# Interleaving the two second-level products of a convolution pair, quarter by quarter

## The chip, the cores and the metric

The kernel runs on one core of one Trainium2 chip. The metric is the device time of one execution in microseconds (us), the median of several. Five engines work at once, each through its own queue of instructions in a fixed order: TensorE (PE) multiplies matrices, VectorE (DVE) and ScalarE (ACT) work element by element, GpSimd (POOL) does a little, and SyncE (SP) issues DMAs. PE writes its products to PSUM, here in banks of 512 float32 columns on 128 partitions.

## What is computed

A decoder layer of two branches over 1024 positions of 1024 channels, all in float32. One large projection makes the inputs of gated linear attention (q, k, v, z_a, gates), of a short gated convolution (cb, cc, xc, z_c) and of the merge (g_a, g_c):

```python
h = rms_norm(x, norm_mix_g)
proj = h @ w_in
q, k, v, z_a, gk_low, cb, cc, xc, z_c, g_a, g_c = split(proj)
o = rms_norm(gla_chunked(q, k, v, gates(gk_low)), gla_norm_g)
y_a = (o * silu(z_a)) @ w_branch_a
u = causal_dwconv(cc * xc, conv_w)              # 3 taps along the sequence
y_c = ((cb * u) * silu(z_c)) @ w_branch_c
merged = sigmoid(g_a + b_ga) * y_a + sigmoid(g_c + b_gc) * y_c
x = x + merged @ w_out
x = x + sigmoid(rms_norm(x, norm_ple_g) @ w_ple_gate) * (p @ w_ple_proj)
return rms_norm(x, norm_final_g)
```

## The kernel before

**Products.** A float32 operand is kept as a high and a low part (hi, lo), and a product of two such operands is three matmuls (`mm3`): hi x hi, lo x hi, hi x lo. The projections are made by a Strassen-Winograd scheme: a `Cell` is 256 columns of one weight, and its eight half-size products become seven, numbered 0 to 6. Each is 12 matmuls of 512 columns, called a wide product here. A cell has three PSUM banks X, Y and V (`cc2X` is bank X of cell cc2). Product 0 is made in X and copied to Y, product 1 in V; products 2, 4 and 6 add to Y, 3 to X, 5 to V. The cells' weight sums are made by DVE in tiles of the tag "T" (four buffers), and split by ACT (a CAST to the high part) and DVE (the low part) into tiles of a ring of six (`RING`, tags whi and wlo).

**The second level.** `Deep(pair, k, turned, pool)` makes product k (0 or 1) of the two cells of a pair together by the same scheme once more: seven quarter products of six matmuls of 256 columns, into the left and right halves of the two cells' banks. Its weight operands are called A, S, T and B (tiles `cc2xc20Ahi`, `cc2xc21Shi` and so on: cells, k, operand, part). Between the quarter products ACT copies halves from bank to bank or into a tile `dw`, and DVE adds. For product 0 this happens in the X banks, for product 1 in the V banks. The convolution has eight pairs: cc0xc0, zc0cb0, cc1xc1, zc1cb1, cc2xc2, zc2cb2, cc3xc3, zc3cb3. The first has a `Deep` for k = 0 alone, the seven others for both. The pairs q0k0 and q1k1 have one for k = 0, the pairs of g_a and g_c one for k = 1. `run(k)` of a `Deep` makes one of its four stretches: quarter product 0; then 4 and 2; then 1; then 3, 5 and 6.

**Order.** `line_up` writes down the order of products: it inserts the stretches of the second level among the wide products of the pair ahead, one wide product or more between two stretches. `run_groups` walks that list and, ahead of each product, loads weight blocks and prepares operands of the coming ones, as far as the ring reaches, by the `slots` that each takes. Every operation is recorded by `Flow` (nearly all rows of the trace carry the line of its call, L508, so rows are told apart by tile names). `set_dues` works out from the end when each must be done, and `put_in_order` takes, for each engine, the most urgent operation that can run. PE's main row keeps the order in which the code names its products. In the finished program a bank is guarded as a whole: an instruction that uses one half waits for an earlier use of the other half by another engine.

Of the kernel before, what the change touches and what calls it, by code (L numbers as in the profile page):

```python
# [16 lines left out]
P = 128  # L17
# [8 lines left out]
RING = 6  # L26
# [493 lines left out]
def kernel(  # L520
# [219 lines left out]
    class Cell:  # L740

        slots = 1

        def __init__(self, name, side, src, res, cons, prods=ORDER, begin=None, s1=None, u2=None, s5=None, fresh=(), mixed=False):
# [7 lines left out]
            (self.steps, self.operand), self.fresh = ring_steps(name, side, self.raw, fresh, mixed), fresh  # L752

# [57 lines left out]
        def run(self, k):  # L811
# [20 lines left out]
            elif k == 2:  # L832
                self.product(2, self.Y, False)
# [24 lines left out]
    class Deep:  # L858

        slots = 4  # L860

        def __init__(self, pair, k, turned, pool):
            self.pair, self.k, self.turned, self.pool, self.ring, self.behind = pair, k, turned, pool, [], []
            self.first = False
            for c in pair:
                c.deep[k] = self
                c.prods = [n for n in c.prods if n != k]
# [3 lines left out]

        def load(self, k):
            for c in self.pair:
                c.load(self.k)

        def prep(self, k):
            if self.ring:
                return
            for c, n in self.behind:
                c.prep(n)  # L880
            self.load(k)
            a, b = (c.operand(self.k) for c in self.pair)
            name = f"{self.pair[0].name}{self.pair[1].name}{self.k}"

            def put(what, src):
                hi = bp.tile([P, 4, P], F32R, tag="whi", name=f"{name}{what}hi", bufs=RING)
                lo = bp.tile([P, 4, P], F32R, tag="wlo", name=f"{name}{what}lo", bufs=RING)
                n = src.shape[1]
                split(hi[:, 0:n, :], lo[:, 0:n, :], src)
                return [(hi[:, m:m + 2, :], lo[:, m:m + 2, :]) for m in range(0, n, 2)]  # L890

            t = [bp.tile([P, 4, P], F32, tag="T", name=f"{name}S{m}", bufs=4) for m in range(2)]
            s1, s2, s3, s4 = (t[m][:, n:n + 2, :] for m in range(2) for n in (0, 2))
            tt(s3, a[:, 0:2, :], b[:, 0:2, :], op=ALU.subtract)
            tt(s1, b[:, 0:2, :], b[:, 2:4, :], op=ALU.add)
            tt(s2, s1, a[:, 0:2, :], op=ALU.subtract)
            tt(s4, a[:, 2:4, :], s2, op=ALU.subtract)
            a11, a12 = put("A", a)
            s1, s2 = put("S", t[0])
            s3, s4 = put("T", t[1])  # L900
            a22, = put("B", b[:, 2:4, :])
            self.ring = [a11, s3, s2, a12, s1, s4, a22]

        def product(self, n, acc, start):
# [8 lines left out]
        def run(self, k):  # L913
            self.prep(k)
            a, b = self.pair
            left, right = slice(0, 256), slice(256, 512)
            if k == (0 if self.first else 2) and self.k:
                for c in self.pair:
                    c.Y = bank(c, 1)
                    nc.scalar.copy(c.Y, c.X if c.seed is None else c.seed)  # L920
            if k == 0:
# [3 lines left out]
            elif k == 1:  # L925
                self.product(4, self.a[:, right], False)
                self.product(2, self.b[:, left], False)
                self.d = [self.pool.tile([P, 256], F32, tag=f"dw{n}", name=f"{a.name}{self.k}dw{n}") for n in range(2)]
                nc.scalar.copy(self.d[0], self.b[:, left])
                nc.scalar.copy(self.d[1], self.a[:, right])  # L930
                tt(self.a[:, right], self.a[:, right], self.d[0], op=ALU.add)
            elif k == 2:
                self.product(1, self.b[:, left], False)
# [1333 lines left out]
```

## Time and profile before

| | us |
|---|---|
| median of 3 runs | 1067.59 (1066.97 to 1067.98) |
| the profiled execution, its own time | 1067.77 |
| its span | 1065.9 |
| PE busy | 1056.9 (99%) |
| DVE busy | 928.9 (87%) |
| ACT busy | 678.1 (64%) |
| POOL busy | 48.9 (5%) |

The span runs from the first to the last instruction that the profiler saw; 1.87 us lie around it. A row of the timeline gives the start, the duration, the engine, and the operation as out<-in. A matmul's duration includes its way through the array, so matmuls overlap: what counts is the distance between two starts, 0.23 us for 512 columns and 0.12 for 256.

### The profile page before, as it was taken

The numbers are of one execution on the slowest core, as the hardware profiler recorded it, in microseconds if no ns is written. First come the engines' busy times: TensorE is split into PE (matmuls) and PEld (weight loads), VectorE is DVE, ScalarE is ACT, GpSimd is POOL, SyncE is SP. The second block draws the span as 40 slices with busy tenths as digits, with TensorE's granted clock in tenths as the row PEclk, the third lists the DMA queues.
The fourth block names the chain that finished last, engine by engine and source line by source line (L and its number), as shares of the span: only waits on it lengthen the run. The fifth ranks groups of instructions, "written<-read, shape, count | busy, mean of one in ns | idle before, by whom it ended". The sixth has DMA issues, their size and how long they took to land.

```text
span 1065.9 us, 16311 instructions
## 1 busy us (share of the span) xinstructions
PE 1056.9 (99%) x5235; PEld 896.7 (84%) x5235; DVE 928.9 (87%) x1576; ACT 678.1 (64%) x1295; POOL 48.9 (5%) x83
## 2 busy tenths in 40 slices
PE   9999999999999999999999999999999999999997
PEld 7888888888888888888888889988888888888886
DVE  6899869968897898889889799997999989899897
ACT  6867768876545656556566478676857535456656
POOL 0000000000000000000000002120000000012221
PEclk9999999999999999999999999999999999999999
DMA  8996468966768666865869879998596879799963
GB/s 311 331 363 217 181 205 280 314 228 230 232 202 284 225 221 213 263 220 182 275 220 322 289 247 323 320 337 315 197 310 229 314 215 318 251 327 326 315 220 142
DMA packets 179269, 280.18 MB, mean 263 GB/s; under 512 B 15728, under 2 KB 84592, under 8 KB 176752
## 3 DMA queue, kind: packets, MB, share of 16 engines
q1 hardware_dynamic: 179040, 278.89, 77.5%
q8 instruction: 41, 0.67, 0.3%
q14 instruction: 44, 0.36, 0.1%
q10 hardware_dynamic: 144, 0.26, 0.1%
HBM read 178.95 MB, written 100.14 MB: 262 GB/s over the span
## 4 chain that ended last, share of the span: by engine, by line
PE 92%; DVE 3%; DMA 1%; ACT 1%; issue 1%; POOL 0%; POOLq 0%; SPq 0%; ACTq 0%
PE pe L508 2%; PE op L508 2%; PE j0Y L508 1%; PE vY L508 1%; PE zY L508 1%; DMA wt<-in_wb_dram 1%; PE j1X L508 1%; PE j0X L508 1%; PE j0V L508 1%; PE kv L508 1%; PE ga1Y L508 1%; PE xc3Y L508 1%; PE cb2Y L508 1%; PE cb1Y L508 1%; PE cb0Y L508 1%; PE cc3Y L508 1%
## 5 line engine op out<-in xcount | busy, mean ns | idle before, releaser
L508 DVE TENSOR_TENSOR wt<-wt 128x256 f32<-128x256 f32 (+1 forms) x48 | 24.6, 513 | 2.1 <-issue 2.0
L508 ACT ACT_TABLE_LOAD x19 | 24.4, 1283 | 1.3 <-PEq L2256 0.7
L508 DVE SCALAR_TENSOR_TENSOR u<-t,vec,u 128x512 f32<-128x512 f32 x32 | 23.9, 754 | 1.1 <-ACT u L508 0.9
L508 ACT ACTIVATE junk<-x 128x512 bf16<-128x512 f32 (+1 forms) x30 | 18.0, 600 | 10.0 <-DVE x L508 8.2
L508 POOL TENSOR_SCALAR rg<-ms 128x1 f32<-128x1 f32 x8 | 10.2, 1275 | 257.0 <-ACT junk L508 256.9
L508 POOL MEMSET t<- 128x2 f32 x8 | 0.8, 99 | 405.6 <-DMA ked<-turned 202.3
L508 ACT ACTIVATE og<-op,or 128x256 f32<-128x256 f32 x32 | 13.4, 472 | 1.8 <-POOL or L508 1.8
L508 ACT ACTIVATE wt<-wt,vec 128x256 f32<-128x256 f32 x32 | 13.8, 501 | 0.0
L508 ACT ACTIVATE oq<-oq,vec 128x512 f32<-128x512 f32 x20 | 13.2, 715 | 0.3 <-DMA oq<-od 0.3
L508 DVE TENSOR_TENSOR vs<-vs 128x512 fp32r<-128x512 f32 x16 | 11.0, 689 | 2.8 <-ACT vs L508 2.7
L508 ACT CAST S<-S 128x512 fp32r<-128x512 f32 x14 | 8.7, 621 | 7.3 <-PE op L508 7.3
L508 ACT ACTIVATE junk<-op 128x256 bf16<-128x256 f32 x32 | 12.2, 382 | 1.4 <-PE op L508 1.3
L508 ACT ACTIVATE u<-t,vec 128x512 f32<-128x512 f32 x16 | 11.6, 725 | 2.3 <-DVE t L508 2.3
L508 PE MATMUL pe<-wpehi,pThi 128*128 128x512 f32 x32 | 13.0, 408 | 0.0
L508 DVE STREAM_TRANSPOSE oT<-szl 128x256 f32<-128x256 f32 x32 | 13.0, 428 | 0.0
L508 PE MATMUL pe<-wpelo,pThi 128*128 128x512 f32 x32 | 12.9, 404 | 0.0
L508 DVE TENSOR_TENSOR s<-y,s 128x512 f32<-128x512 f32 x16 | 11.0, 689 | 2.2 <-DMA vs<-vd 1.2
L508 PE MATMUL op<-v,aTh 128*128 128x256 f32 x64 | 12.7, 282 | 0.0
L508 ACT CAST vs<-vs 128x512 fp32r<-128x512 f32 x16 | 9.9, 621 | 3.9 <-DMA vs<-vd 3.7
L508 POOL TENSOR_TENSOR or<-or,mhalf 128x2 f32<-128x2 f32 x16 | 12.2, 761 | 1.3
L508 PE MATMUL pe<-wpehi,pTlo 128*128 128x512 f32 x32 | 12.0, 390 | 0.0
L508 DVE SCALAR_TENSOR_TENSOR S<-S,dds,kv 128x256 f32<-128x256 f32 x24 | 10.4, 473 | 1.4 <-PE kv L508 1.2
(4252 smaller groups left out, 4393.6 us busy)
## 6 DMA issues: line engine op xcount, KB each, us to landing
wtd<-wt SPq DMA_DIRECT2D x88, 128.0 KB, 3.0
wt<-in_wb_dram SPq DMA_DIRECT2D x16, 512.0 KB, 5.1
vsd<-vs SPq DMA_DIRECT2D x16, 512.0 KB, 4.2
v<-vsd SPq DMA_DIRECT2D x16, 512.0 KB, 5.6
wgq<-wtd SPq DMA_DIRECT2D x7, 1024.0 KB, 6.5
vraw<-in_wv_dram SPq DMA_DIRECT2D x24, 256.0 KB, 4.1
zraw<-in_wv_dram SPq DMA_DIRECT2D x20, 256.0 KB, 5.1
uq<-ud SPq DMA_DIRECT2D x5, 1024.0 KB, 6.8
```

Source lines behind the costliest of these rows:

```text
L508: o.call(*[place(a) for a in o.args], **{k: place(a) for k, a in o.kw.items()})
```

## The change

`Deep` is split into `begin` (the weight sums), `put` (one operand into the ring) and `step(n)`, one of six steps: 0 is quarter product 0 and the copy of its half bank, 1 is quarter product 4 and a copy to a tile d5, 2 is quarter product 2, a copy to a tile dw and an add, 3 is quarter product 1 and an add, 4 is quarter products 3 and 5, 5 is quarter product 6. A new class `Duo` holds both parts (k = 0 and k = 1) of a pair and makes each step for the one and then for the other, steps 0 to 2 in a first stretch and 3 to 5 in a second. `line_up` puts the first stretch ahead of the last wide product (6) of the pair ahead's first cell and the second ahead of that of its second cell. A `Deep` that is alone has three stretches, (0), (1, 2) and (3, 4, 5). The copy into bank Y moves into product 2 of the cell. A T operand of the first part lies in a tile outside the ring (xhi, xlo), and both B operands share one ring tile. Quarter products, copies and adds are the same in number.

```diff
         def load(self, k):
             for n in NEED[self.side][k]:
@@ -830,6 +831,9 @@
                 if self.X is not None:
                     self.join()
             elif k == 2:
+                if self.Y is None:
+                    self.Y = bank(self, 1)
+                    nc.scalar.copy(self.Y, self.X if self.seed is None else self.seed)
                 self.product(2, self.Y, False)
...
+        def __init__(self, pair, k, turned, pool, home=None):
+            self.pair, self.k, self.turned, self.pool, self.home, self.behind = pair, k, turned, pool, home or pool, []
...
+        def slots(self, k):
+            return 0 if k else 4
...
+        def begin(self):
+            self.load(0)
+            self.ab = a, b = [c.operand(self.k) for c in self.pair]
+            self.t = t = [bp.tile([P, 4, P], F32, tag="T", name=f"{self.name}S{m}", bufs=4) for m in range(2)]
+            s1, s2, s3, s4 = (t[m][:, n:n + 2, :] for m in range(2) for n in (0, 2))
+            tt(s3, a[:, 0:2, :], b[:, 0:2, :], op=ALU.subtract)
+            tt(s1, b[:, 0:2, :], b[:, 2:4, :], op=ALU.add)
+            tt(s2, s1, a[:, 0:2, :], op=ALU.subtract)
+            tt(s4, a[:, 2:4, :], s2, op=ALU.subtract)
+
+        def put(self, what, left, right=None, extra=None):
+            src = {"A": self.ab[0], "S": self.t[0], "T": self.t[1], "B": self.ab[1][:, 2:4, :]}[what]
+            hi = (extra or bp).tile([P, 4, P], F32R, tag="xhi" if extra else "whi", name=f"{self.name}{what}hi", bufs=1 if extra else RING)
+            lo = (extra or bp).tile([P, 4, P], F32R, tag="xlo" if extra else "wlo", name=f"{self.name}{what}lo", bufs=1 if extra else RING)
+            n = src.shape[1]
+            split(hi[:, 0:n, :], lo[:, 0:n, :], src)
+            self.ring[left] = hi[:, 0:2, :], lo[:, 0:2, :]
+            if right is not None:
+                self.ring[right] = hi[:, 2:4, :], lo[:, 2:4, :]
+            return hi, lo
...
-        def run(self, k):
-            self.prep(k)
+        def step(self, n):
             a, b = self.pair
             left, right = slice(0, 256), slice(256, 512)
-            if k == (0 if self.first else 2) and self.k:
-                for c in self.pair:
-                    c.Y = bank(c, 1)
-                    nc.scalar.copy(c.Y, c.X if c.seed is None else c.seed)
-            if k == 0:
+            if n == 0:
                 self.a, self.b = bank(a, 2 * self.k), bank(b, 2 * self.k)
                 self.product(0, self.a[:, left], True)
                 nc.scalar.copy(self.b[:, left], self.a[:, left])
-            elif k == 1:
-                self.product(4, self.a[:, right], False)
-                self.product(2, self.b[:, left], False)
-                self.d = [self.pool.tile([P, 256], F32, tag=f"dw{n}", name=f"{a.name}{self.k}dw{n}") for n in range(2)]
-                nc.scalar.copy(self.d[0], self.b[:, left])
-                nc.scalar.copy(self.d[1], self.a[:, right])
-                tt(self.a[:, right], self.a[:, right], self.d[0], op=ALU.add)
-            elif k == 2:
-                self.product(1, self.b[:, left], False)
-                tt(self.b[:, right], self.b[:, left], self.d[1], op=ALU.add)
+            elif n == 1:
+                self.product(4, self.a[:, right])
+                self.d5 = self.home.tile([P, 256], F32, tag="d5", name=f"{self.name}d5")
+                nc.scalar.copy(self.d5, self.a[:, right])
+            elif n == 2:
+                self.product(2, self.b[:, left])
+                d = self.pool.tile([P, 256], F32, tag="dw", name=f"{self.name}d")
+                nc.scalar.copy(d, self.b[:, left])
+                tt(self.a[:, right], self.a[:, right], d, op=ALU.add)
+            elif n == 3:
+                self.product(1, self.b[:, left])
+                tt(self.b[:, right], self.b[:, left], self.d5, op=ALU.add)
+            elif n == 4:
+                self.product(3, self.a[:, left])
+                self.product(5, self.a[:, right])
             else:
-                self.product(3, self.a[:, left], False)
-                self.product(5, self.a[:, right], False)
-                self.product(6, self.b[:, left], False)
+                self.product(6, self.b[:, left])
                 for c, t in ((a, self.a), (b, self.b)):
                     if self.k:
                         c.V = t
@@ -945,11 +952,55 @@
                     if c.joined:
                         if c.Y is not None:
                             c.join()
-                    elif 1 not in c.deep:
-                        c.Y = bank(c, 1)
-                        nc.scalar.copy(c.Y, c.X)
                     if c.after:
                         c.after(self.k)
+
+        def run(self, k):
+            self.prep(k)
+            for n in ((0,), (1, 2), (3, 4, 5))[k]:
+                self.step(n)
+
+    class Duo:
+
+        def __init__(self, pair, pool):
+            self.pair, self.pool, self.parts, self.behind, self.at = pair, pool, [pair[0].deep[k] for k in range(2)], [], 0
+
+        def ready(self, k):
+            return True
+
+        def slots(self, k):
+            return 2 if k else 6
+
+        def load(self, k):
+            for c in self.pair:
+                c.load(0)
+                c.load(1)
...
+        def prep(self, k):
+            d, e = self.parts
+            if self.at == 0:
+                self.at = 1
+                d.begin()
+                d.put("A", 0, 3)
+                d.put("S", 4, 2)
+                d.put("T", 1, 5, self.pool)
+                for c, n in self.behind:
+                    c.prep(n)
+                e.begin()
+                e.put("A", 0, 3)
+                e.put("S", 4, 2)
+            if k and self.at == 1:
+                self.at = 2
+                e.put("T", 1, 5)
+                hi, lo = d.put("B", 6)
+                split(hi[:, 2:4, :], lo[:, 2:4, :], e.ab[1][:, 2:4, :])
+                e.ring[6] = hi[:, 2:4, :], lo[:, 2:4, :]
+
+        def run(self, k):
+            self.prep(k)
+            for n in ((0, 1, 2), (3, 4, 5))[k]:
+                for d in self.parts:
+                    d.step(n)
...
+            deep, at = g[0].deep, len(todo)
             if g[0].joined:
-                for n, m in enumerate((3, 5, 7, 8)):
-                    own.insert(m, (g[0].deep[0], n))
-            elif g[0].deep and 0 not in g[0].deep and not todo:
-                g[0].deep[1].first = True
+                for n, m in enumerate((3, 5, 7)):
+                    own.insert(m, (deep[0], n))
+            elif deep and 0 not in deep and not todo:
                 own.insert(2, own.pop(4))
-                for n, m in enumerate((0, 2, 4, 5)):
-                    own.insert(m, (g[0].deep[1], n))
-            elif g[0].deep and 0 not in g[0].deep:
-                at = len(todo)
-                g[0].deep[1].behind = [(c, j) for c, j in todo[-2:] if j == 6]
+                for n, m in enumerate((0, 2, 4)):
+                    own.insert(m, (deep[1], n))
+            elif deep and len(deep) == 1:
+                k, = deep
+                deep[k].behind = [(c, j) for c, j in todo[-2:] if j == 6 and k]
                 for n in range(3):
-                    todo.insert(at - 2 + 2 * n, (g[0].deep[1], n))
-                own.insert(0, (g[0].deep[1], 3))
-            elif g[0].deep and 1 not in g[0].deep:
-                at = len(todo)
-                for n in range(3):
-                    todo.insert(at - 3 + 2 * n, (g[0].deep[0], n))
-                own.insert(1, (g[0].deep[0], 3))
-            elif g[0].deep:
-                at = len(todo)
-                g[0].deep[1].behind = [(c, j) for c, j in todo[-2:] if j == 6]
-                for m, (k, n, left) in enumerate(((0, 0, 5), (0, 1, 4), (0, 2, 3), (0, 3, 2), (1, 0, 2), (1, 1, 1), (1, 2, 0))):
-                    todo.insert(at - left + m, (g[0].deep[k], n))
-                own.insert(1, (g[0].deep[1], 3))
+                    todo.insert(at - (2 if k else 3) + 2 * n, (deep[k], n))
+            elif deep:
+                duo = g[0].duo
+                duo.behind = [(c, j) for c, j in todo[-2:] if j == 6]
+                for n in range(2):
+                    todo.insert(at - 2 + 2 * n, (duo, n))
             todo += own
...
-                met = set()
                 for cc, kk in seq[n:]:
-                    if cc not in met:
-                        reach -= cc.slots
-                    if cc.slots > 1:
-                        met.add(cc)
+                    reach -= cc.slots(kk)
...
-                Deep(g, k, turned[k], tq)
+                Deep(g, k, turned[k], tq, None if k or g[0] is convs[0][0] or g not in convs else vp)
+        for g in convs[1:]:
+            g[0].duo = Duo(g, vp)
```

PE's row at the first stretch of the pair cc2xc2: `cc2xc20A` is operand A of k = 0 and `cc2xc21A` that of k = 1; `h0`, `h1` and `turned0` hold the activations, and cb1 is a cell of the pair ahead. In before:

```order
L508 MATMUL cc2X<-h0hi,cc2xc20Ahi 128x256
L508 MATMUL cc2X<-h0lo,cc2xc20Ahi 128x256
L508 MATMUL cc2X<-h0hi,cc2xc20Alo 128x256
L508 MATMUL cb1V<-h5hi,cb1hi 128x512
L508 MATMUL cb1V<-h5lo,cb1hi 128x512
L508 MATMUL cb1V<-h5hi,cb1lo 128x512
```

(nine more matmuls of cb1V follow, and then the first of S, `cc2X<-turned0h,cc2xc20Shi`). In after:

```order
L508 MATMUL cc2X<-h0hi,cc2xc20Ahi 128x256
L508 MATMUL cc2X<-h0lo,cc2xc20Ahi 128x256
L508 MATMUL cc2X<-h0hi,cc2xc20Alo 128x256
L508 MATMUL cc2V<-h1hi,cc2xc21Ahi 128x256
L508 MATMUL cc2V<-h1lo,cc2xc21Ahi 128x256
L508 MATMUL cc2V<-h1hi,cc2xc21Alo 128x256
L508 MATMUL cc2V<-h1hi,cc2xc21Ahi 128x256
L508 MATMUL cc2V<-h1lo,cc2xc21Ahi 128x256
L508 MATMUL cc2V<-h1hi,cc2xc21Alo 128x256
L508 MATMUL cc2X<-turned0h,cc2xc20Shi 128x256
```

The wide product of cb1V has gone from between A and S, and six matmuls of the other part stand there.

ACT's row around the copy of that first half bank, `xc2X<-cc2X`; `wt` are weights of a later projection that ACT scales, `s` is a gate of the pair ahead. In before:

```order
L508 CAST cb1hi<-cb1raw_4435 128x512
L508 CAST zc1hi<-zc1T_4875 128x512
L508 COPY xc2X<-cc2X 128x256
L508 ACTIVATE wt_1_0_4906<-wt_1_0_4906,vec 128x256 x4
L508 ACTIVATE s_0_1_4986<-zc1u_4816 128x512
```

In after:

```order
L508 CAST cc2xc21Ahi<-cc2T_4955 128x512
L508 ACTIVATE wt_1_0_4985<-wt_1_0_4985,vec 128x256 x3
L508 CAST cc2xc21Shi<-cc2xc21S_5014 128x512
L508 ACTIVATE wt_1_0_4985<-wt_1_0_4985,vec 128x256
L508 ACTIVATE s_1_1_5063<-zc1s_4776 128x512
L508 COPY xc2X<-cc2X 128x256
L508 COPY xc2V<-cc2V 128x256
```

The split of the other part's S and two ACTIVATE now stand directly ahead of the copy, and the copy of the V bank behind it.

ACT's row at the copy that fills the Y bank of the second cell of the pair zc2cb2, `cb2Y<-cb2X`. In before:

```order
L508 ACTIVATE wt_2_256_5537<-wt_2_256_5537,vec 128x256 x4
L508 COPY zc21dw_5626<-cb2V 128x256
L508 COPY zc2Y<-zc2X 128x512
L508 COPY zc21dw_5636<-zc2V 128x256
L508 CAST cb2hi<-cb2T_5609 128x512
L508 CAST zc2hi<-zc2raw_5334 128x512
L508 COPY cb2Y<-cb2X 128x512
```

In after:

```order
L508 CAST zc2hi<-zc2raw_5234 128x512
L508 COPY cb2s_5688<-cb2V 128x512
L508 CAST cb2hi<-cb2raw_5243 128x512
L508 ACTIVATE wt_2_256_5635<-wt_2_256_5635,vec 128x256 x4
L508 COPY cb2Y<-cb2X 128x512
```

The four ACTIVATE of wt have come to stand directly ahead of that copy.

## Rows read from the trace of the kernel before

**Rows 1.** The page's part 1: busy time, share, instructions of each engine.

```profile
span 1065.9 us, 16311 instructions
PE 1056.9 (99%) x5235; PEld 896.7 (84%) x5235; DVE 928.9 (87%) x1576; ACT 678.1 (64%) x1295; POOL 48.9 (5%) x83
```

**Rows 2.** Busy time by stretch: us, engines (x instructions), granted clock, DMA share, GB/s.

```profile
300.00:350.00 50.00, 50.00 (x266) 43.17 (x265) 42.73 (x84) 27.31 (x56) 0.20 (x2) 1.00 0.69 225
450.00:500.00 50.00, 50.00 (x280) 43.74 (x279) 44.93 (x87) 31.02 (x68) 0.00 (x0) 1.00 0.65 215
```

**Rows 3.** All waits of PE: us in total, times, longest.

```profile
PE warm L508 <- DVE zero L508: 1.0, 1, 1.0
PE zY L508 <- DVE zp L508: 0.2, 1, 0.2
```

**Rows 4.** Chain of waits, 425 to 460 us: start, us, engine, tile.

```profile
435.02 2.72 PE zc1X L508 x12
437.74 2.72 PE cb1X L508 x12
440.46 2.72 PE zc1V L508 x12
443.18 0.71 PE cc2X L508 x6
443.89 2.75 PE cb1V L508 x12
446.64 0.72 PE cc2X L508 x6
447.36 0.72 PE xc2X L508 x6
448.08 2.76 PE zc1Y L508 x12
450.84 0.72 PE xc2X L508 x6
451.56 2.76 PE cb1Y L508 x12
```

**Rows 5.** Timeline at a half bank's copy: start, us, engine, operation, [idle before, releaser].

```profile
331.08 0.69 DVE L508 TENSOR_TENSOR cc0u<-cc0V,cc0u 128x512 f32<-128x512 f32 x1
331.09 0.28 PE L508 MATMUL zc0X<-h0hi,zc0cb00Alo 128*128 128x256 f32 x1
...
331.41 0.36 ACT L508 COPY cb0X<-zc0X 128x256 f32<-128x256 f32 x1 [0.26 <-PE zc0X L508]
...
331.68 0.68 DVE L508 TENSOR_TENSOR cc0lo<-cc0T,cc0hi 128x512 fp32r<-128x512 f32 x1
```

**Rows 6.** Timeline of ACT behind the copy xc2X<-cc2X.

```profile
444.20 1.71 ACT L508 ACTIVATE wt<-wt,vec 128x256 f32<-128x256 f32 x4
445.81 0.62 ACT L508 ACTIVATE s<-zc1u 128x512 f32<-128x512 f32 x1
```

**Rows 7.** Timeline of ACT around the pair zc2cb2, 495 to 504 us.

```profile
495.58 0.61 ACT L508 CAST zc2cb21Thi<-zc2cb21S 128x512 fp32r<-128x512 f32 x1
496.10 0.40 ACT L508 CAST zc2cb21Bhi<-cb2T 128x256 fp32r<-128x256 f32 x1
...
503.05 0.57 ACT L508 COPY cb2Y<-cb2X 128x512 f32<-128x512 f32 x1 [0.97 <-DVE t L508]
```

**Rows 8.** Timeline at a matmul that waited for an ACT copy, 134 to 136 us.

```profile
134.25 1.12 ACT L508 COPY vY<-j0c 128x512 f32<-128x512 f32 x2
...
134.91 0.50 PE L508 MATMUL vY<-v_0hi,h2hi 128*128 128x512 f32 x1
...
135.25 0.39 PE L508 MATMUL vY<-v_0lo,h2hi 128*128 128x512 f32 x1
...
135.48 0.40 PE L508 MATMUL vY<-v_0hi,h2lo 128*128 128x512 f32 x1
```

**Rows 9.** Tile cc2raw, 400 to 460 us: its loads, first reader, time to land.

```profile
L508 SPq DMA_DIRECT2D cc2raw<-in_wc_dram x4: 333/385/1027, 409.0 to 437.7; - x4
L508 DVE TENSOR_TENSOR cc2xc20S<-cc2raw,xc2raw x1: 434/434/434, 422.7 to 422.7; 128x256 f32<-128x256 f32 x1
...
DMA to landing us min/median/max: 2.8/3.3/6.4
```

More of the change, by code (lines that the diff above doesn't have):

```diff
@@ L740 @@
     class Cell:
-        slots = 1
         def __init__(self, name, side, src, res, cons, prods=ORDER, begin=None, s1=None, u2=None, s5=None, fresh=(), mixed=False):
@@ L752, in __init__ @@
             (self.steps, self.operand), self.fresh = ring_steps(name, side, self.raw, fresh, mixed), fresh
+        def slots(self, k):
+            return 1
         def load(self, k):
@@ L858 @@
     class Deep:
[L860 to L864, printed above, removed]
+        def __init__(self, pair, k, turned, pool, home=None):
+            self.pair, self.k, self.turned, self.pool, self.home, self.behind = pair, k, turned, pool, home or pool, []
+            self.name, self.ring = f"{pair[0].name}{pair[1].name}{k}", {}
             for c in pair:
@@ L880, in prep, with product @@
                 c.prep(n)
[L881 to L904, printed above, removed]
+            self.begin()
+            self.put("A", 0, 3)
+            self.put("S", 4, 2)
+            self.put("T", 1, 5)
+            self.put("B", 6)
+        def product(self, n, acc, start=False):
             shi, slo = self.ring[n]
@@ L947, in run, with slots @@
                             c.join()
-                    elif 1 not in c.deep:
-                        c.Y = bank(c, 1)
-                        nc.scalar.copy(c.Y, c.X)
                     if c.after:
                         c.after(self.k)
+        def run(self, k):
[7 more added lines that the diff above has]
+            return True
+        def slots(self, k):
+            return 2 if k else 6
[27 more added lines that the diff above has]
+                    d.step(n)
     def line_up(groups):
```

## The prediction, made before the changed kernel had run

> **What bounds the kernel now.** First the page's part 1: TensorE (PE) works for 1056.9 of the 1065.9 us of the span, VectorE (DVE) 87% of it, ScalarE (ACT) 64% [rows 1]. The stretches say the same of the places that the change touches: 50.00 of 50 us of PE in each of two stretches of the convolution pairs, at a granted clock of 1.00, with 44.93 us of DVE at most and some 30 of ACT [rows 2]. The list of waits has two for all of PE, 1.0 us at the start and 0.2 later [rows 3]. So the kernel is a chain of matmuls laid end to end; no wait that the change could remove is worth anything, and the time moves in two ways only: the same matmuls take another time because they follow each other differently, or PE begins to wait. Both are small sums against 1067 us, and a measurement of this kernel can tell some 0.2% (2.1 us) from no change.
>
> **The order of matmuls.** The chain of waits is read next, because its pieces are rows of PE work with nothing between them [rows 4]. A product of 12 matmuls of 512 columns takes 2.72 us where another such follows (435.02, 437.74, 440.46). The same product takes 2.75 or 2.76 where it follows a stretch of quarter products (443.89, 448.08, 451.56), and six matmuls of 256 columns take 0.72 inside a stretch and 0.71 or 0.72 as its first (443.18). Leaving a stretch thus costs 0.03 to 0.04, and entering one gives back 0 to 0.01. The change makes the same 5060 matmuls. By the program's order 86 stretches of 256-column matmuls become 49: seven per pair become two for the seven pairs with both second-level products, four become three for the single ones. The sum: 37 x 0.03 = **1.1 us less**. The ends are 37 x (0.03 - 0.01) = 0.75 and 37 x 0.04 = 1.5. What makes the difference the rows don't say, only that it stands behind every stretch.
>
> **The new close place.** In before, A of a part (its first quarter product, into the left half of a bank) is followed by a wide product, and S (into the right half of the same bank) comes 2.72 us later. In after, S comes behind the A of the other part only, 0.72 us later. Between the two ACT copies the left half to the other cell's bank, and in the program S waits for ACT. Rows 5 give the chain. Let T0 be the start of A's last matmul. The copy starts 0.32 later (331.09 to 331.41) and lasts 0.36 [rows 5]. What follows an ACT write that PE waits for is shown once [rows 8]: two copies take 1.12 together, so the first ends near 134.82, and the matmul starts at 134.91, 0.09 later, with its successor 0.34 behind it where 0.23 is usual (0.11 more, as the first weight load isn't hidden there). S can thus be going at T0 + 0.32 + 0.36 + 0.09 + 0.11 = T0 + 0.88, and the order would have it at T0 + 7 x 0.12 = T0 + 0.84. That is 0.04 late with ACT idle, and whatever ACT is busy with at T0 + 0.32 comes on top. The second part's copy has 0.72 more and is covered by the delay of the first, so one wait per pair counts, seven in all.
>
> What stands ahead of the copy in ACT's order decides its size. The split of S itself (a CAST of 512 columns) is released by the second-last matmul of the wide product ahead, at T0 - 1.05. With the lag of rows 5 and 0.11 for the longer matmul it starts at T0 - 0.63; such operations follow one another at 0.52 (495.58 to 496.10) [rows 7], so ACT is free at T0 - 0.11.
> - zc0cb0, cc1xc1, cc3xc3, zc3cb3: nothing long behind that CAST: 0.04 each, 0.16.
> - zc1cb1: two ACTIVATE of wt (four take 1.61, from 444.20 to 445.81, so 0.40 each [rows 6]): free at T0 + 0.69 to 0.75; 0.04 + 0.43 = 0.47.
> - cc2xc2: one ACTIVATE of wt and one of s (0.62 [rows 6]): free at T0 + 0.9; about 0.6.
> - zc2cb2: a tiny copy and a CAST of 512 columns: free at T0 + 0.55; 0.27.
>
> Together 1.5 us. Each of the three long ones can fall away, if ACT reaches those operations earlier than this, or grow by one more operation of 0.52: 0.3 to 3.0. I take 1.5, since the order of each engine is fixed and rows 6 and 7 have the durations.
>
> The copy of a first product into a second cell's Y bank moves too. In before a wide product and quarter products lay between the last use of that bank by the pair ahead and this copy's user; in after one wide product, 2.72. For cb2Y ACT has a CAST and four ACTIVATE of wt to do ahead of it: 0.52 + 1.61 + 0.57 for the copy itself [rows 6, 7] + 0.20 to get PE going = 2.90, against 2.72: 0.2 late, between 0 and one operation more, 0.7. At xc3Y the four wt stand ahead of that CAST and are done while the CAST waits for its ring tile, and elsewhere there are at most three, 0.40 less: nothing.
>
> **What else moves and why I cost it at nothing.** DVE does the same 1579 operations; they move together, ahead of each pair. Its neighbours in a row start 0.60 apart (331.08, 331.68) [rows 5], and over 50 us it has 5 us free [rows 2]. If that cover were gone, a pair would pay an operation, 0.60. The two B blocks share a ring tile, and the second S to be turned has one outside the ring: no operation more. SP issues the loads of weight blocks for both parts of a pair at once. Those of this pair were issued from 409.0 and first used by DVE at 422.7, and landed 3.3 us after issue, 6.4 at most [rows 9], so a load that comes a product (2.72) later than now is still there in time. From 750 us on PE's order is the same; there neither gain nor cost.
>
> **The sum.** -1.1 + 1.5 + 0.2 = +0.6 us. On the profiled run, 1067.77 us (span 1065.9 and 1.87 around it), that is 1068.4; that run stands 0.18 above the median of 1067.59, so for the median I say **1068.2**. With the ends: -1.5 + 0.3 + 0 = -1.2 and -0.75 + 3.0 + 0.7 = +3.0; the likely part of it, with not all ends on one side, is 1066.9 to 1069.7.
>
> The Trainium skill bears on the close place (PSUM — Partial Sum Buffer, section PSUM bank collisions raise a hardware error): it asks to guard PSUM by bank and quadrant, in the simple version by bank, and not by address. That speaks against the change, since the two halves of a bank differ in address alone and S must wait for the copy; by a guard by address the sum would be -1.1, 1066.5, and no row of before shows which.
>
> **The rivals.**
> *No wait (1066.5).* ACT is done with its other work before T0 + 0.32 everywhere and the 0.04 lie inside what PE's queue bridges. For it: ACT is busy for 31.02 of 50 us only [rows 2], and the order of one engine doesn't say when it reaches a place. Against it: the chain is 0.04 too long even with ACT idle. Time: 1067.6 - 1.1 = 1066.5, and 1066.1 at the far end of the gain. Chance 0.16.
> *ACT in the way everywhere (slower).* The close place is hit in both parts of each of seven pairs, each time by one operation of 0.52 that is in progress: 14 x 0.5 = 7 - 1.1: 1073.5. For it: ACT is busy 55 to 62% of the time [rows 2], and the list holds such operations near the copies of at least three pairs. Against it: in four pairs nothing long stands ahead, and a wait in a pair's first part gives its second part time. It decides from 3.2 us of waits, six or seven places of the 14. Chance 0.11.
> *Operands late (slower).* DVE prepares two parts at once and the last of T is one operation late in each pair: 7 x 0.60 = 4.2 - 1.1 + 0.6 of the waits above: 1071.3. For it: 87% busy [rows 1]. Against it: 5 us free of 50, and all operands of the second stretch have a wide product more. Chance 0.05.
> *It does not do what it says.* If the planner had spread the parts again, the time would be the old one, 1067.6. The order of after has the two parts in turn in all seven pairs, so 0.02.
>
> **How the numbers follow.** My forecast of waits of 1.7 against a gain of 1.1 has 0.66. The range of 1066.0 to 1069.9 takes in the forecast's likely part and the case without waits, 0.82 in all, and leaves out the two slower ones. Faster by over 0.2% (under 1065.5) needs a gain greater than any row shows: 0.04. Slower by over 0.2% (over 1069.7) is the two slower rivals and a rest of the forecast's upper end: 0.11 + 0.05 + 0.03 = 0.19. Within 0.2%: 0.77.
>
> **What the profile of after would show.** The gain: fewer products of 2.75 or 2.76 in the chain, and 2.72 in their place. The waits: in the chain's pieces a first part's A and S of cc2xc2, zc1cb1 and zc2cb2 that take 0.3 to 0.6 longer than 0.72 each, with S released by ACT's copy, and the ACTIVATE rows directly ahead of that copy; PE's list of waits no longer two lines. If the four other pairs show more than 0.1 each, my ACT order is misread; if there is no ACT wait at all, a guard by bank doesn't hold S up. PE rows that wait for DVE, or a wait for a load, would speak for the third rival. The prediction is wrong if PE's busy time for the same matmuls changes by more than 1.5 us, or if a place after 750 us moves.

## The result and the profile after

| | before | after |
|---|---|---|
| median of 22 runs each, us | 1067.26 | 1068.99 |
| lowest to highest | 1066.55 to 1068.60 | 1068.36 to 1070.20 |
| the profiled execution, its own time | 1067.77 | 1068.60 |
| its span | 1065.9 | 1066.8 |

The ratio is 1.0016, with a 95% interval of 1.0010 to 1.0023: some 1.7 us slower, about the least that can be told from no change. The prediction was 1068.2 in a range of 1066.0 to 1069.9, with "within 0.2%" at 0.77; so time and range held. Its two terms were both too small, and the larger error was in the waits. One of the eleven times of the first experiment, 1779.01 us at a mean granted clock of 0.556 where the ten others have 0.997 to 0.999, belongs to a slower state and is left out of its median below.

The page's part 1 of after, to be read beside [rows 1]: the same work in a longer span.

```profile
span 1066.8 us, 16329 instructions
PE 1056.5 (99%) x5235; PEld 896.8 (84%) x5235; DVE 929.6 (87%) x1576; ACT 679.0 (64%) x1295; POOL 52.1 (5%) x83
```

The two stretches of [rows 2] in after, same columns:

```profile
300.00:350.00 50.00, 50.00 (x274) 43.47 (x273) 43.67 (x82) 27.46 (x56) 0.20 (x2) 1.00 0.64 209
450.00:500.00 50.00, 49.07 (x288) 43.32 (x287) 44.09 (x85) 32.76 (x73) 0.10 (x1) 1.00 0.68 222
```

In the second PE is no longer busy throughout: 0.93 us of 50 are missing. The list of all waits of PE in after (total, times, longest) says for whom; before had two lines [rows 3]:

```profile
PE warm L508 <- DVE zero L508: 1.0, 1, 1.0
PE zc2X L508 <- ACT cb2X L508: 0.6, 1, 0.6
PE cc2X L508 <- ACT xc2X L508: 0.3, 1, 0.3
PE zc1X L508 <- ACT cb1X L508: 0.2, 1, 0.2
```

Three first parts of pairs, and each time the ACT copy of the half bank. The list counts from the end of a matmul, which overlaps the next; from start to start the matmul was 0.79, 0.46 and 0.40 late, and its successor 0.10 more. The chain of waits at cc2xc2 (start, us, what) shows the place, and answers to [rows 4]:

```profile
434.24 2.72 PE zc1X L508 x12
...
442.40 2.72 PE cb1V L508 x12
445.12 2.72 PE zc1Y L508 x12
...
450.94 0.51 ACT wt L508
451.45 0.52 ACT s L508
451.97 0.28 ACT xc2X L508
452.25 0.04 issue
452.29 0.97 PE cc2X L508 x6
453.26 0.72 PE cc2V L508 x6
```

Two things are to be seen: the wide products ahead take 2.72 each, none of them 2.75 or 2.76, since no stretch lies between them any more; and ACT's wt, s and copy follow one another on the path, as the order had them. S then takes 0.97 in place of 0.72.

**Both terms can be read from one period.** From the first quarter product of one pair to that of the next the traces show (first starts of the pairs zc0cb0, cc1xc1, zc1cb1, cc2xc2, zc2cb2, cc3xc3, zc3cb3; us):

| kernel | zc0 to cc1 | to zc1 | to cc2 | to zc2 | to cc3 | to zc3 | first q0V to first yc0V |
|---|---|---|---|---|---|---|---|
| before, 7 stretches a pair | 37.51 | 37.51 | 37.51 | 37.51 | 37.51 | 37.51 | 527.93 |
| after, 2 stretches | 37.49 | 37.25 | 37.73 | 37.81 | 38.37 | 37.25 | 529.11 |
| after, once more | 37.75 | 37.25 | 37.73 | 37.81 | 38.37 | 37.25 | 529.40 |
| two stretches, urgent | 37.25 | 37.25 | 37.21 | 37.33 | 37.85 | 37.41 | 527.21 |
| three stretches, urgent | 37.30 | 37.30 | 37.30 | 37.30 | 37.30 | 37.68 | 527.20 |

Where nothing waits, a pair takes 37.51 with seven stretches, 37.30 with three and 37.25 with two: 0.05 for every stretch less. That is 0.26 a pair and 1.8 us for seven pairs. After's excess over 37.25 is 0.24 + 0 + 0.48 + 0.56 + 1.12 + 0 = 2.4, and 0.27 more at zc3cb3, whose matmuls were late by 0.07, 0.11 and 0.10. So 2.7 - 1.8 = +0.9; two single parts ahead of the pairs (q1k1 and cc0xc0) lose a stretch each, another 0.1. That agrees with the traces: from the first matmul of q0V to the last of cb3 before takes 376.17 and after 376.92, +0.75. The whole middle part, from the first matmul of q0V to the first of yc0V, grew by 529.11 - 527.93 = 1.2; the 0.44 left lie behind the pairs, where the order of the attention's rows has changed too (the seventh experiment has the same there). Ahead of q0V traces of one kernel differ by 0.2, those of all kernels by 1.2, and behind the last matmul one finds 7.87 to 8.32 in kernels with the same tail. That is why single profiles (+0.8) and medians (+1.7) stand apart, and why I compare the middle part.

### The profile page after: what moved, and what is told of

Read it like the earlier page. It is cut to its first block, busy times and chain, and to the rows that moved or that the text cites. A ratio compares the mean times of both kernels' runs of the same rounds, so it can differ in the third digit from the quotient of the medians.

```text
span 1066.8 us, 16329 instructions
## 1 busy us (share of the span) xinstructions
PE 1056.5 (99%) x5235; PEld 896.8 (84%) x5235; DVE 929.6 (87%) x1576; ACT 679.0 (64%) x1295; POOL 52.1 (5%) x83
## 4 chain that ended last, share of the span: by engine, by line
PE 93%; DVE 3%; DMA 1%; ACT 1%; issue 1%; POOL 0%; POOLq 0%; DVEq 0%; ACTq 0%; SPq 0%
PE zY L508 3%; PE vY L508 3%; PE pe L508 2%; PE op L508 2%; PE j0Y L508 1%; PE j1X L508 1%; PE zV L508 1%; PE j0V L508 1%; PE j0X L508 1%; PE kv L508 1%; PE cb2Y L508 1%; PE ga0Y L508 1%; PE ga2Y L508 1%; PE ga1Y L508 1%; PE q0Y L508 1%
## 5 line engine op out<-in xcount | busy, mean ns | idle before, releaser
L508 POOL TENSOR_SCALAR or<-oms 128x2 f32<-128x2 f32 x16 | 7.9, 495 | 120.5 <-ACT junk L508 120.5
L508 DVE TENSOR_TENSOR x<-x,pe 128x512 f32<-128x512 f32 (+1 forms) x18 | 11.1, 628 | 0.3
```

The lines of the kernel that those rows point to most:

```text
L508: o.call(*[place(a) for a in o.args], **{k: place(a) for k, a in o.kw.items()})
```

## The experiments

My theory: the change saves something for every stretch that is left out, and loses it again since ACT's copy of a half bank, standing behind other ACT work, holds up S. The rivals: DVE makes the operands of two parts too late; the waits are an accident; a way out of a stretch costs nothing. All times are medians beside runs of before on the same chip.

| run | us | before, us | ratio (95% interval) | stretches | middle part |
|---|---|---|---|---|---|
| e1 after once more | 1069.27 | 1067.31 | 1.0017 (1.0008 to 1.0027) | 50 | 529.40 |
| e2 three stretches, first try | 1113.79 | 1067.31 | 1.0433 (1.0419 to 1.0447) | 57 | 572.94 |
| e3 no scaling of wt | 1066.85 | 1067.31 | 0.9997 (0.9988 to 1.0006) | 50 | 527.36 |
| e4 copy twice | 1070.82 | 1067.31 | 1.0033 (1.0021 to 1.0045) | 50 | 530.41 |
| e5 three stretches, own tiles | 1067.88 | 1067.73 | 1.0001 (0.9992 to 1.0010) | 57 | 528.13 |
| e6 part by part | 1078.44 (one) | 1067.73 | - | 50 | 539.11 |
| e7 before, copy twice | 1068.01 (one) | 1067.73 | - | 87 | 528.35 |
| e8 two stretches, urgent | 1065.89 | 1067.40 | 0.9988 (0.9979 to 0.9997) | 50 | 527.21 |
| e9 three stretches, urgent | 1067.02 | 1067.40 | 0.9995 (0.9986 to 1.0004) | 57 | 527.20 |

(Before: 88 stretches, middle part 527.93. The prediction counted 86 and 49, 37 less; this count has 88 and 50, 38 less.)

### e1: the changed kernel once more

> The changed kernel once more, unaltered. Theory (the copies of half banks hold up the second quarter products, because ACT is at other work): the order of every engine is fixed, so the waits of PE at zc1, cc2 and zc2 come back within 0.1 us each, and the time is 1.4 to 2.0 us above before. Rival (the added time is an accident of DMA and differs from run to run): other places wait, or the three waits differ by 0.3 and more.

Measured 1.96 us above before. The waits at zc1, cc2 and zc2 came back to 0.01 (0.40, 0.46 and 0.79 from start to start). One place varied: the second part at zc0cb0 was 0.13 late in the first trace and 0.39 here. ACT's timeline of the two, after first, shows why (start, us, operation, [idle before, releaser]):

```profile
339.69 0.19 ACT L508 COPY t<-end 128x2 f32<-128x2 f32 x1 [0.49 <-DVE u L508]
339.79 0.37 ACT L508 COPY cb0V<-zc0V 128x256 f32<-128x256 f32 x1
```

```profile
340.16 0.19 ACT L508 COPY t<-end 128x2 f32<-128x2 f32 x1 [0.75 <-DVE u L508]
340.26 0.37 ACT L508 COPY cb0V<-zc0V 128x256 f32<-128x256 f32 x1
```

The half bank's copy stands behind a copy of two columns that itself waits for DVE: idle for 0.49 and 0.75 us, with PE waiting behind it. So the three large waits are fixed by the order, and a smaller one hangs on when DVE gets there.

### e2 and e5: a wide product between A and S

Both parts still in turn, but in three stretches:

```diff
-            for n in ((0, 1, 2), (3, 4, 5))[k]:
+            for n in ((0,), (1, 2), (3, 4, 5))[k]:
...
-                for n in range(2):
-                    todo.insert(at - 2 + 2 * n, (duo, n))
+                for n in range(3):
+                    todo.insert(at - 3 + 2 * n, (duo, n))
```

> Both parts in turn as in the change, but in three stretches (steps 0; 1 and 2; 3 to 5), with a wide product between A and S and between S and T. By the order it has 57 quarter stretches (before 88, after 50). Theory: the copy of a half bank has 2.7 us more, so the waits at A and S (2.3 us in the three long ones) are gone, and the fewer ways out of a stretch stay: 31 x 0.044 = 1.4 us less than before, 1066 where before is 1067.3. The T operand of the first part now needs a ring tile that comes free with the last product 4 of the pair ahead; if that is late, a wait at step 3 shows it, and the time is up to 2 us more. Rival (the operands of two parts, prepared by DVE at once, are late): the waits at S stay, since DVE has the same work, and the time stays 1 us or more above before.

The first try, 46 us slower, tells nothing of the copies: PE waited 2.7 to 3.2 us at every pair for the CAST of the second part's S, which my edit had put behind operands of later products (at zc3cb3 DVE takes the first part's T at 603.98, and sums for the second part's S only from 605.18 on). The second try gave the second part's weight sums tiles of their own (in `begin`: `(own or bp).tile(..., tag="xT" if own else "T", bufs=2 if own else 4)`) and prepared one product less ahead of them.

> Three stretches for both parts in turn again (0; 1 and 2; 3 to 5, a wide product between A and S and between S and T), but without the mistake of the run before this one: the second part's weight sums have tiles of their own in place of the tile outside the ring, and only the products that come between are prepared ahead of its operands. 57 quarter stretches (before 88, after 50). Theory: no copy of a half bank is waited for (each has 2.7 us more), and S of the second part is ready in time; 31 x 0.044 = 1.4 us less than before: 1065.9 where before is 1067.3, 3 us less than after. Rival (two parts' operands at once are too much for DVE): waits for DVE's low parts at S and T of 0.3 and more in each of the seven pairs, 1068 and above. Rival (a way out of a stretch costs nothing in itself): no waits, and before's time.

Five of the six periods are 37.30, 0.21 less than before's, and no pair waits at A and S, except cc2xc2: its period is 38.61. PE's one wait in the list beside that at the start, the chain there, and ACT at the second part's half bank:

```profile
PE xc2X L508 <- DVE cc2xc20Tlo L508: 0.5, 1, 0.5
```

```profile
457.17 0.42 DVE wt L508
457.59 0.61 DVE cc2xc20Tlo L508
458.20 0.04 issue
458.24 0.74 PE xc2X L508 x4
```

```profile
450.31 1.71 ACT L508 ACTIVATE wt<-wt,vec 128x256 f32<-128x256 f32 x4
451.93 0.36 ACT L508 COPY xc2V<-cc2V 128x256 f32<-128x256 f32 x1
```

So the copies' waits go with the wide product at six of the seven pairs, and the gain per stretch is there, but one pair gives 1.3 back: 0.76, since the low part of T stood behind subtractions of wt on DVE; 0.37 at the second part's S (too short for the list), since the copy of its half bank stood behind four ACTIVATE of wt on ACT, in spite of the wide product; 0.1 at xc2Y. The expected 1.4 us came to nothing: 1.0001, for beside the 1.3 the 0.44 behind the pairs is here too. The rival of late DVE operands holds at one pair of seven.

### e3: ACT without the scaling of wt

```diff
-                    soon(act, q, q, AF.Copy, scale=gple[:, k:k + 1])
+                    pass
```

> The changed kernel without ACT's scaling of the wt weights (32 ACTIVATE of 128x256 left out, so later products are made with unscaled weights). Theory: by the order one CAST alone stands ahead of the copy at zc1 and cc2, so these waits fall from 0.5 to 0.1 or 0.2 each, zc2 falls from 1.0 to some 0.5 as the CAST of vs leaves that place, the Y bank of cb2 waits no more (0.1): 1.3 to 1.5 us less than after, about before + 0.3. Rival (DVE's operands are late): the waits stay, after's time. Rival (the time comes from something outside these places): after's time, with the waits gone.

2.4 us below after's median in e1, on the same chip. PE's one wait beside that at the start:

```profile
PE zc3X L508 <- ACT cb3X L508: 0.4, 1, 0.4
```

The waits at zc1, cc2, zc2 and the Y bank of cb2 are gone altogether (I had left some 0.8 of them, which is most of why it gained 2.4 and not 1.5), and zc3cb3 got one of 0.6 with a CAST of vs ahead of its copy; 0.2 stay at the second part of zc0cb0, of the kind seen in e1. DVE had the same work as in after, and PE waited for none of its operands. The plain matmul rows of this run and of before give the price of a stretch: the first A of cc2xc2 and of zc2cb2 are 37.51 apart in before and 37.25 here.

```profile
443.02 0.28 PE L508 MATMUL cc2X<-h0hi,cc2xc20Ahi 128*128 128x256 f32 x1
...
480.53 0.28 PE L508 MATMUL zc2X<-h0hi,zc2cb20Ahi 128*128 128x256 f32 x1
```

```profile
450.12 0.28 PE L508 MATMUL cc2X<-h0hi,cc2xc20Ahi 128*128 128x256 f32 x1
...
487.37 0.28 PE L508 MATMUL zc2X<-h0hi,zc2cb20Ahi 128*128 128x256 f32 x1
```

### e4 and e7: the copy twice, in after and in before

```diff
                 nc.scalar.copy(self.b[:, left], self.a[:, left])
+                nc.scalar.copy(self.b[:, left], self.a[:, left])
```

> The changed kernel with the copy of the first half bank issued twice, the same values to the same place, in all parts. A second copy of 128x256 ends 0.27 to 0.30 later. By the order the ACTIVATE of wt and s have moved away from the copies at zc1 and cc2, and one CAST stands ahead of both copies at every pair. Theory: each of the seven pairs waits 0.25 to 0.4 at the first S (cc1 and cc3, which waited for nothing, too), in all 2 to 2.8 us, so after's time within 0.7 us, shared out otherwise; the single parts, where a wide product lies between A and S, wait for nothing. Rival (DVE's operands): cc1 and cc3 still wait for nothing, and zc2 and cc2 wait as before.

Every one of the seven pairs waited at the first S: 0.28 at cc1, cc2, zc2 and cc3, and 0.37, 0.53 and 0.46 at zc0, zc1 and zc3, each with 0.10 more for the next matmul. cc1 and cc3 had no wait in after, and cc2 and zc2 now waited for less, because the order had moved ACT's other work away. The chain at cc1xc1:

```profile
375.22 0.73 PE cc1X L508 x6
375.95 0.02 issue
375.97 0.36 ACT xc1X L508
376.34 0.02 issue
376.36 0.36 ACT xc1X L508
376.73 0.04 issue
376.77 0.97 PE cc1X L508 x6
```

The two copies are the whole path from A to S. Two places that I had not named waited too, 0.4 each: the second part's S at zc1cb1 and its T at cc3xc3, where PE waited for a copy into d. The time, 3.5 us above before, is more than I expected of the total (after's time within 0.7) and more than the 2.5 of the middle part; the trace is of the fastest of the six executions, 1069.32.

> The kernel before with the copy of the first half bank issued twice, as the control of the run with the doubled copy: here a wide product lies between A and S. Theory: ACT has 2.7 us for both copies, so no wait at any pair and before's time within 0.5 us. Rival (the doubled copy costs time in another way, by ACT's load): 2 to 3 us above before, as in the changed kernel with the doubled copy.

In before, where a wide product follows A, the six periods stayed 37.51 and the time was 0.3 above: the doubled copy costs nothing there. The 0.42 by which the middle part grew lies behind the pairs, in single late matmuls of ga3V and of the attention's first rows that after has as well; this kernel has the same order there.

### e6: one part after the other

```diff
-            for n in ((0, 1, 2), (3, 4, 5))[k]:
-                for d in self.parts:
+            for d in self.parts:
+                for n in ((0, 1, 2), (3, 4, 5))[k]:
                     d.step(n)
```

> The changed kernel with the steps of the two parts one part after the other inside each stretch (steps 0, 1, 2 of the first, then of the second), so S comes directly behind A of the same bank. Theory (S waits for the copy of the other half of its bank, which takes T0 + 0.77 to T0 + 0.88 even with ACT idle): every one of the 14 places waits, 0.65 to 0.75 with ACT idle plus 0.1 for the first weight load, and those with an operation ahead more: 14 x 0.75 to 1.0 = 10 to 14 us above a kernel without waits, 1076 to 1080. Rival (the copy is not what S waits for, S's operands are): the waits are those of after, and the time is after's.

All 14 places waited, 0.61 to 1.68 from start to start and 0.10 more each, and the time rose by 10.7 us, within the range. With ACT idle, at cc1xc1:

```profile
377.96 0.72 PE cc1X L508 x6
378.68 0.02 issue
378.71 0.36 ACT xc1X L508
379.07 0.04 issue
379.12 0.97 PE cc1X L508 x6
```

A's last matmul started at 378.39 (T0). The copy begins at T0 + 0.32 and S at T0 + 0.73, a little earlier than the 0.77 to 0.88 that I had expected: a price for the chain that the trace of before could not show in one piece.

### e8 and e9: the same order of products, with the parts' work made urgent

Only the due times of the two parts' operands (and in e8 of their copies and adds) are set earlier, so that ACT and DVE take them first; in e9 on top of e5, with 10 us and for the operands alone.

```diff
         def prep(self, k):
+            nc.hurry = 65.0
+            self.ready_operands(k)
+            nc.hurry = 0.0
...
                 for d in self.parts:
+                    nc.hurry = 65.0
                     d.step(n)
+                    nc.hurry = 0.0
```

> The changed kernel, its two stretches and its PE order of the pairs kept; only the operands, copies and adds of the two parts are given an earlier due time (65 us), so that ACT and DVE take them ahead of other work that is ready. By the order the copies now stand directly behind the CAST of S at five of the seven pairs (no ACTIVATE of wt, no CAST of vs between), and at cc3xc3 one ACTIVATE of s lies between. Theory: the waits at zc1, cc2 and zc2 (2.0 us with their second 0.1) shrink to 0.4 or less together, cc3xc3 gets one of 0.4; with 38 fewer ways out of a stretch, 38 x 0.04 = 1.5 us less, 0.3 to 1.0 us below before. Rival (two copies and two parts are simply too much for ACT there, whatever the order): waits of 2 us and more stay, at the same three pairs or others, and the time stays 1 us or more above before.

1.5 us below before (0.9979 to 0.9997) and some 3 below after: the only version here that beats both, and by more than the 0.3 to 1.0 that I had expected. PE's one wait beside that at the start, and ACT at zc1cb1, where after had two ACTIVATE of wt ahead of the copy:

```profile
PE zc2X L508 <- ACT cb2X L508: 0.3, 1, 0.3
```

```profile
411.94 0.62 ACT L508 CAST zc1cb11Shi<-zc1cb11S 128x512 fp32r<-128x512 f32 x1 [0.86 <-PE xc1Y L508]
412.88 0.36 ACT L508 COPY cb1X<-zc1X 128x256 f32<-128x256 f32 x1 [0.32 <-PE zc1X L508]
413.60 0.36 ACT L508 COPY cb1V<-zc1V 128x256 f32<-128x256 f32 x1 [0.36 <-PE zc1V L508]
```

At zc1cb1 the copies now wait for PE, not PE for them. The stretches and PE's order of the pairs are the change's own, so what made the change slower was where the helpers' other work stood, not the two stretches; that it was ACT's follows from e3, for the due times of e8 move DVE's work too. What is left is zc2cb2 (0.44 and 0.11, a little over the 0.4 expected of the three places together), 0.16 at cc3xc3, where I had expected 0.4, and 0.1 each at two second parts. The middle part is 0.7 shorter than before's; of the 1.5 by the medians the rest lies ahead of it and behind, where single traces vary by as much.

> The three stretches with tiles of their own (57 stretches), the operands of both parts given a due time 10 us earlier. In that run PE waited for DVE's low part of T at cc2xc2 (0.75 us with its second 0.1) and for a copy there (0.36), behind subtractions of wt that had the earlier due time. Theory: these waits go, and the time is 31 x 0.044 = 1.4 us below before, less some 0.3 for the rest: 0.8 to 1.4 us below. Rival (DVE is full at cc2xc2, and the lateness moves to another of its results): a wait of 0.5 and more at another operand there, and before's time.

The wait at cc2xc2 went (its period is 37.30), one of 0.38 came at cc3xc3 (for an ACT copy that had itself waited for an add on DVE), and the gain was 0.4 us where I had expected 0.8 to 1.4. Its middle part is as short as that of e8, so the 1.1 us between their medians lies elsewhere, and I did not follow it further.

## Why the prediction was right, and where its sizes were off

- **What bounds the kernel: right.** No wait was removed, and nearly the whole change is the sum of two small terms on PE. Neither of the last two signs of being wrong showed: PE's busy time changed by 0.4 us, and from the first matmul of yc0V, behind 750 us, to the last of all both traces take 299.38. (The prediction's counts, 5060 matmuls and 1579 operations of DVE, are not the page's, which has 5235 and 1576 before and after; no term rests on them.)
- **Ways out of a stretch: right in kind, too small.** I read 0.03 from one view whose rows have two digits, and counted an entry as a gain. (What the 2.72 of 440.46 shares with the two other such rows is a wide product ahead of it; behind it stands a stretch.) The periods give 0.05 for every stretch less: 1.8 us for the pairs and 0.1 for two single parts, not 1.1. Matmul by matmul it can be seen that in before and after the first nine wide ones behind a stretch (in e9 the first five) start 0.228 to 0.235 apart on the average of each place, and all later ones 0.227. But that is not all of it: from cc1xc1 to zc1cb1 the 120 wide matmuls take 27.46 us in before and 27.27 in after and e9, the 84 of 256 columns 10.05, 9.98 and 10.03. So 0.19 of the 0.26 lie in the wide ones and 0.07 in the short ones, where I had a loss of up to 0.01 a stretch. The trace of before alone would not have given the larger number: 120 x 0.227 + 84 x 0.120 = 37.32, 0.19 below its period, is 0.03 for each of seven stretches again. It takes the period of a second order.
- **The close place: right, and it decided the sign.** Copies hold up S at just the pairs that the order named. cc2xc2: 0.56 with the second matmul (forecast 0.6). zc1cb1: 0.50 (0.47). cb2Y: 0.16 by its product of 2.88 in place of 2.72 (0.2).
- **zc2cb2: the step that failed.** I let the CAST of S start at T0 - 0.63, when its ring tile comes free. ACT was not free then. Its timeline in after, and the matmul that waited (T0 is 488.80):

```profile
488.46 0.62 ACT L508 COPY t<-cc2s 128x512 f32<-128x512 f32 x1
488.98 0.62 ACT L508 CAST zc2cb21Shi<-zc2cb21S 128x512 fp32r<-128x512 f32 x1
489.50 0.19 ACT L508 COPY t<-end 128x2 f32<-128x2 f32 x1
489.60 0.61 ACT L508 CAST vs<-vs 128x512 fp32r<-128x512 f32 x1
490.12 0.36 ACT L508 COPY cb2X<-zc2X 128x256 f32<-128x256 f32 x1
```

```profile
490.53 0.39 PE L508 MATMUL zc2X<-turned0h,zc2cb20Shi 128*128 128x256 f32 x1 [0.63 <-ACT cb2X L508]
```

  The CAST started at T0 + 0.18, behind a copy of 512 columns that I had not counted, and two CASTs then stood ahead of the half bank's copy: 0.9 us with the successor, where I had 0.27. The period has 0.1 more in the second part's A, whose low part DVE had ended at 489.11 for a matmul of 489.16.
- **The 0.04 with ACT idle: wrong.** cc1xc1 and cc3xc3 waited for nothing. I had added to the chain the 0.11 by which a matmul is slow once it has waited, and 0.09 for a step from copy to matmul that takes 0.05 in e6; by e6 S can start at T0 + 0.73, which is 0.11 before it is due at T0 + 0.84.
- **The second part is covered by the first: wrong at zc0cb0 and zc3cb3.** Where the first copy is in time or nearly so, there is no delay to hide behind, and an operation between the two copies (a wait for DVE; a CAST of vs) shows: 0.24 to 0.5 and 0.1. At zc3cb3 the first S was 0.18 late as well: as at zc2cb2 a copy of 512 columns stood ahead of the CAST of S, which began at T0 - 0.12. Both pairs are above the 0.1 that the prediction named as the sign that its ACT order is misread.
- **What I did not count:** 0.44 behind the pairs, from the attention's rows in another order. e7 has the same there without the change to the pairs.
- **The rivals.** "No wait" fell. "ACT in the way everywhere" had the mechanism and the wrong number of places: three large ones and three small, 2.7 us in all, below the 3.2 from which I had let it decide. "Operands late" fell for the change (e3) and shows at one pair in e5. The sum was 2.7 - 1.9 + 0.4 = 1.2 in the middle part of that trace, 1.5 in e1, against +0.6 forecast; errors of 0.8 in the gain and 1.0 and more in the waits went against each other. That the time came out so near the forecast is in part luck.

For the rule of the Trainium skill that the prediction weighed (PSUM — Partial Sum Buffer, section PSUM bank collisions raise a hardware error: guard by bank and quadrant, in the simple version by bank, not by address): the traces agree that S waits for a copy of the other half of its bank, in e6 at all 14 places. That is what this program's waits do; whether the chip itself would need them no run here shows.

What stays open: why the first wide matmuls behind a stretch are slower by up to 0.008 us each. Only its size is shown, and that it needs no stretch: behind the short waits at cb2Y (after and e1) and at xc2Y (e5), with wide products on both sides, the next four to six matmuls start 0.228 to 0.236 apart too.

## What to carry to other kernels

On an engine that never waits, two orders of the same instructions differ by their transitions, here by 0.05 us each. A single row has too few digits for that, and the period of one order taken apart gave the same 0.03; the periods of two orders beside each other show it. Before two dependent steps are moved closer, work out the chain between them with its engine idle, and then read what stands ahead of each link in that engine's order, including instructions that wait themselves. If the chain is tight, order the helper's work first: the same change was 1.7 us slower with other ACT work ahead of the copies, and 1.5 us faster than before (0.3 to 2.2 by its interval) with it behind them.

## What the runs showed of the hardware

- With ACT idle (e6) a copy of 128x256 from one half of a bank begins 0.32 after the start of the last matmul into it and lets the next matmul start at 0.73; behind a wait the next start is 0.22 away and not 0.12, each time.
- Waits of 0.4 to 1.7 us left the granted clock at 1.00 in the stretches read. In e2, at zc3cb3, PE stood still for 2.9 us up to 606.76; the granted clock was 1.00 ahead of that (598.00 to 603.90) and half of it (1.2 of 2.4 GHz) when PE went on, for over 6 us. The stretches there (us, then engines, granted clock, DMA share, GB/s):

```profile
606.80:607.90 1.10, 0.81 (x3) 0.52 (x3) 1.10 (x4) 0.00 (x0) 0.00 (x0) 0.50 0.00 0
608.20:613.00 4.80, 4.80 (x20) 4.51 (x20) 3.52 (x7) 1.64 (x4) 0.31 (x1) 0.50 0.14 55
613.50:618.00 4.50, 4.50 (x33) 4.23 (x32) 2.12 (x6) 1.85 (x5) 0.31 (x1) 1.00 0.40 132
```

  Matmuls of 256 columns started 0.21 apart there in place of 0.12. PE's waits as listed add up to some 26 us in the pairs of e2, and the middle part grew by 45. The list counts less than the distance of the starts, as above, and by the granted clock in stretches about each of the seven long waits TensorE had half the clock for some 34 us in all: a late operand costs more than its own time once the clock falls.
